# A hybrid decoder layer: mixer and filling work emitted step by step, with the q, k, v and pool projections woven into the top-key search

## The chip, the core and the metric

The kernel runs on one core of a Trainium2 chip. The metric is device microseconds of one execution. The core has five engines that matter here: TensorE (PE in the profile, with its weight loads as PEld), VectorE (DVE), ScalarE (ACT), GpSimd (POOL) and SyncE (SP), which issues most of the DMAs. The engines run side by side, each through its own queue in order, and meet at semaphores.

## What is computed

One layer over 1,024 tokens of width 1,024, in float32:

```python
x = x + 0.5 * swiglu(rms_norm(x, ffn1_norm), ffn1_w_gate, ffn1_w_up, ffn1_w_down)   # width 2816
h = rms_norm(x, mix_norm)
q, k, v, qi, ki, wi, u = split(h @ w_in)           # 512, 512, 512, 256, 64, 4, 512 columns
q, k = rope(rms_norm(q)), rope(rms_norm(k))        # 8 heads of 64
score[t, s] = sum_h wi[t, h] * relu(qi[t, h] . ki[s])   # 4 index heads, causal
attn = softmax attention of each query over its 256 best keys by score
pooled = (trailing mean over 2/4/8/16 tokens - token) @ pool_w * pool_scale   # 4 channel groups, from u
x = x + concat(attn, pooled) @ w_out
x = x + 0.5 * swiglu(rms_norm(x, ffn2_norm), ffn2_w_gate, ffn2_w_up, ffn2_w_down)
```

## The kernel before, in words

The 1,024 tokens are worked on in two halves of 512. Every float32 operand of a matmul is split into a high and a low part, and a product is three matmuls (`mm3`, lines 65 to 68; all of them are recorded under line 63). The parts are made by `split`: a copy on ScalarE and a subtraction on VectorE or GpSimd.

The program goes through these stages (lines 797 to 816):

1. The first FFN's gate and up products for both halves at once (`norm_blocks`, `expand`), with the mixer's weights split beside them into DRAM pieces (`make_piece`).
2. `down(0)`: the first FFN's down projection of half 0, alone. In groups of four 128-wide slices of the hidden width, `down_group` (line 354) loads and splits weights, and sums twelve matmuls into a bank of the tag `fg` for each of four token tiles and two column halves.
3. `mixer(0, "A")`, the mixer of half 0.
4. `norm_transposed(0, 2, "A")`, the norm ahead of the second FFN of half 0.
5. `down(1)`, 6. `mixer(1, "B")`, 7. the norm of half 1, 8. `ffn(0)`, the whole second FFN of half 0, 9. `ffn(1)`.

A mixer (line 772) does, in this order: a transposing norm into four buffers `XA` or `XB` (two for the high parts, two for the low ones); the index projection with its rotary step (`index_proj`); the scores of those token tiles that have more than 256 keys to choose from (`scores`; two tiles in half 0, four in half 1); the pooling mixer (`pool_mixer`); the projections of v, k and q (`v_proj`, `qk_proj`), which go to DRAM; the search for the 256th best score (`top_masks`); attention; the output projection (`out_proj`).

`proj` (line 449) takes four PSUM banks, two of the tag `ba` and two of `bt`, one for each token tile, and for each of eight weight pieces does 12 matmuls. `qk_proj` copies each bank into an `sc` tile, computes the norm over each head and rotates: line 511 multiplies by the norm on GpSimd, 513 by the cosine on VectorE, 514 and 515 by the sine on GpSimd, 516 adds on GpSimd; line 519 transposes on TensorE.

`top_masks` is a bitwise search, 31 steps one after the other: half of the tiles are counted against a threshold on VectorE (`count`, line 621) and half on ScalarE (line 641), and two small VectorE operations (647, 648) make the next threshold. In each softmax step of attention (line 699) two tiles of 128 queries are scored, the mask added, exponentiated on ScalarE (715) and scaled on VectorE (719); the transposes and products with v of a step (`values`) are emitted one step later. Each finished head pair is split and written to DRAM (lines 762 to 768), and `out_proj` reads all of it back in four pairs of 128 rows, the attention's last pair as the last.

What sets the order: the program is written for a tile framework. Each tile has a tag with a number of buffers (`BUFS`, `PBUFS`, lines 46 to 48: `sc` 4, `mk` 6, `bw` 3, `XA` 4, `XB` 4, `x8` 4, `ba` 2, `bt` 2, `fg` 3, `pv` 1), and waits where none is free. The framework orders the instructions at compile time by a simulated time line; an instruction emitted earlier has priority, and `high_priority` lifts one above the rest. `split_shared` (line 337) gives the subtraction to VectorE where `alone[0]` is set, otherwise two of three to GpSimd; `ffn` does likewise at line 423.

Of the kernel before, what the change touches and what calls it, by code (L numbers as in the profile page):

```python
# [37 lines left out]
def hybrid_layer(ctx: ExitStack, tc: tile.TileContext, x, ffn1_norm, ffn1_w_gate, ffn1_w_up,  # L38
# [111 lines left out]
    def norm_transposed(h, which, region):  # L150
        hT = [t("X" + region, [128, 4, HALF], F32R) for j in range(4)]
        xn = [normed(h, i) for i in range(4)]
        for k in range(NK):
            ps = bank(("ba", "bt")[k % 2])
# [199 lines left out]
    def down_group(h, gr, acts, wd, scale, done=None):  # L354
        n = len(gr)
        for c in range(2):
            cols = slice(c * 512, (c + 1) * 512)
            wts = down_weights(wd, gr, c)
            for i in range(4):
# [10 lines left out]
                if done is not None and gr[-1] == NF - 1:  # L370
                    r0 = h * HALF + i * 128
                    nc.sync.dma_start(done[0, r0:r0 + 128, cols], xo)

    def down(h, a_in, wd):
        for gr in GROUPS:
# [8 lines left out]
            down_group(h, gr, acts, wd, 1.0)  # L384


    def ffn(h, hT, wg, wu, wd, done):
# [18 lines left out]
        for gr in GROUPS:  # L406
            acts = []
            for ff in range(gr[0], gr[-1] + 1, 2):
                s2 = []
                for pg in expand2(ff, wg):  # L410
# [3 lines left out]
                    s2.append(s)  # L414
                if pend is not None:
                    down_group(*pend)
                    pend = None
                for s, pu in zip(s2, expand2(ff, wu)):
# [5 lines left out]
                    acts.append(a)  # L424
            pend = (h, gr, acts, wd, 0.5, done)
        down_group(*pend)


    def out_proj(h, region):
        fetch_x(h)  # L430
        mt = [None] * 4
        for j in (2, 3, 0, 1):
            mt[j] = t("X" + region, [128, 2, 2, HALF], F32R)
            nc.gpsimd.dma_start(mt[j].rearrange("p k l c -> p k (l c)"),
                                m_dr[h][2 * j:2 * j + 2].rearrange("k p l c -> p k (l c)"))
        for c in range(2):
            banks = [bank(tag, "op") for tag in ("ba", "ba", "bt", "bt")]
            for n, k in enumerate((4, 5, 6, 7, 0, 1, 2, 3)):
                wt = get_piece(P_O + 2 * k + c)
                m = mt[k // 2][:, k % 2]  # L440
                for i in range(4):
                    tok = slice(i * 128, (i + 1) * 128)
                    mm3(banks[i], m[:, 0, tok], m[:, 1, tok], wt[:, 0], wt[:, 1], n == 0, n == NK - 1)
# [5 lines left out]
    def proj(hT, first, n):  # L449
        hi, lo = hT  # L450
        banks = [bank(tag, "pj") for tag in ("ba", "ba", "bt", "bt")]
        for k in range(NK):
            wt = get_piece(first + k, n)
            for i in range(4):
                tok = slice(i * 128, (i + 1) * 128)
                mm3(banks[i][:, :n], hi[k][:, tok], lo[k][:, tok], wt[:, 0], wt[:, 1], k == 0, k == NK - 1)
# [7 lines left out]
    def index_proj(h, hT, cs):  # L464
        banks = proj(hT, P_I, N_I)
        for i in range(4):
# [29 lines left out]
            nc.vector.tensor_sub(k2[64:], pk[64:], f(k2[64:]))  # L496

    def qk_proj(h, hT, cs, which):
        banks = proj(hT, P_QKV + 8 * which, 512)
        for i in range(4):  # L500
# [5 lines left out]
            nc.scalar.copy(s[:, 512:], banks[i])  # L506
# [4 lines left out]
            nc.gpsimd.tensor_mul(n, n, r[:, :, None].to_broadcast([128, NH, HD]))  # L511
# [4 lines left out]
            nc.gpsimd.tensor_add(o, o, m)  # L516
# [6 lines left out]
            for l, v in enumerate((hi, lo)):  # L523
# [4 lines left out]
                nc.sync.dma_start(dst.rearrange("a p c -> p a c"), f(v).rearrange("p (a c) -> p a c", a=4))  # L528

    def v_proj(h, hT):  # L530
        banks = proj(hT, P_QKV + 16, 512)
        for i in range(4):
# [3 lines left out]
            for l, v in enumerate((hi, lo)):  # L536
                nc.sync.dma_start(v_dr[h * HALF + i * 128:h * HALF + (i + 1) * 128, :, l], f(v).rearrange("p (h d) -> p h d", d=HD))

    def pool_mixer(h, hT):
        hi, lo = hT  # L540
        tiles = []
        for g in range(4):
# [38 lines left out]
            nc.sync.dma_start(m_dr[h][4 + g], f(m))  # L581

    def scores(h, i, sc):
# [5 lines left out]
        for c0 in range(0, n2, 512):  # L589
            cw = min(512, n2 - c0)  # L590
            o = sc[:, c0:c0 + cw]
            for hd in range(4):
# [6 lines left out]
                else:  # L599
                    r = t("mk", [128, 512])  # L600
                    nc.scalar.activation(r[:, :cw], b[:, :cw], AF.Relu)
                    nc.vector.scalar_tensor_tensor(o, r[:, :cw], w, o, op0=ALU.mult, op1=ALU.add)
        d = sc[:, g * 128:(g + 1) * 128]
        nc.vector.scalar_tensor_tensor(d, diag, DIAG, d, op0=ALU.mult, op1=ALU.add)

    def top_masks(h, tiles, sc, masks):
# [32 lines left out]
        for bit in range(30, -1, -1):  # L639
# [5 lines left out]
            for j in range(d):  # L645
# [3 lines left out]
                                           op1=ALU.bitwise_xor)  # L649
        nc.vector.tensor_scalar(th[:, act], f(c[:, act]), -1.0, None, op0=ALU.mult)  # L650
# [10 lines left out]
        for j in range(m):  # L661
# [7 lines left out]
            if n2 > n:  # L669
                nc.gpsimd.memset(masks[j][:, n:n2], NEG)  # L670

# [7 lines left out]
    def attention(h, masks, region):  # L679
# [19 lines left out]
        def softmax(hd, ql, nk, ks, qt):  # L699
# [18 lines left out]
            for ti in range(2):  # L718
# [135 lines left out]
```

## Time and profile before

| | |
|---|---|
| time of three runs | 2051.86, 2048.58, 2051.59 us (median 2051.59) |
| the profiled execution's own time | 2051.53 us |
| its span, first to last instruction | 2049.7 us |
| mean granted TensorE clock | 0.967 |
| busy, TensorE | 1913.4 us |
| busy, VectorE / ScalarE / GpSimd | 1146.2 / 800.6 / 648.9 us |

The span is what the rows of the profile add up to; the time of the execution is 1.8 us longer. Rows of the kind "stage" give the length of a stretch of the span, the busy time of an engine in it with its number of instructions, and the clock granted to TensorE; the length less the busy time is that engine's idle time.

### The profile page before, as it was taken

What the parts mean: (1) busy time and instruction counts of PE and PEld (TensorE: products, weight loads), DVE (VectorE), ACT (ScalarE), POOL (GpSimd) and SP (SyncE); (2) the same over time, 40 slices, a digit from 0 to 9 for tenths busy, and PEclk for the clock granted to TensorE, in tenths of its full rate; (3) what the DMA queues carried; (4) which work ended last, traced back from release to release, by engine and by line L of the source; (5) the groups of instructions that cost most, each with busy time, mean ns of one, the idle gap of its engine ahead of it and who ended that gap; (6) DMA issues with size and microseconds to landing.
All of it is one profiled execution on the core that took longest, in us unless ns stands there. A gap on an engine that the chain in (4) does not pass through costs nothing.

```text
span 2049.7 us, 24399 instructions
## 1 busy us (share of the span) xinstructions
PE 1913.4 (93%) x8640; PEld 1566.5 (76%) x8640; DVE 1146.2 (56%) x2038; ACT 800.6 (39%) x1490; POOL 648.9 (32%) x609
## 2 busy tenths in 40 slices
PE   4999999999999999748799999999999889999999
PEld 2788888887888777536588888787888668888887
DVE  7656656654564693357133689536768523444344
ACT  6343333332333352235143377433565413222331
POOL 6545545520022451752123333675332010000000
PEclk8999999999999999969899999999999899999999
DMA  4366656657455547677536337485555433333332
GB/s 127 114 199 202 206 157 198 220 197 280 136 193 171 137 131 211 206 133 196 188 99 170 101 100 227 127 229 137 134 134 164 145 124 102 91 95 93 92 113 72
DMA packets 223050, 315.26 MB, mean 154 GB/s; under 512 B 34128, under 2 KB 141776, under 8 KB 222928
## 3 DMA queue, kind: packets, MB, share of 16 engines
q1 hardware_dynamic: 204304, 281.19, 43.5%
q0 software_dynamic: 18624, 32.51, 7.6%
q8 instruction: 68, 1.11, 0.2%
q14 instruction: 54, 0.44, 0.1%
HBM read 242.84 MB, written 70.81 MB: 153 GB/s over the span
## 4 chain that ended last, share of the span: by engine, by line
PE 72%; DVE 10%; ACT 5%; POOL 5%; issue 4%; DMA 3%; SPq 0%; POOLq 0%; ACTq 0%; DVEq 0%
PE fg L63 28%; PE dn L63 18%; PE bt L63 6%; PE ba L63 5%; PE pv L63 4%; PE pj L63 4%; PE op L63 3%; ACT x L641 2%; DVE x L622 2%; PE tp L733 1%; PE lg L63 1%; PE pu L63 1%; DVE sel L647 1%; DMA rawd<-in_ffn_w_down_dram 1%; POOL st L137 1%
## 5 line engine op out<-in xcount | busy, mean ns | idle before, releaser
L63 PE MATMUL dn<-wd,a 128*128 128x512 f32 x2112 | 510.1, 396 | 10.4 <-DVE x L367 4.5
L63 PEld LDWEIGHTS dn<-wd,a 128*128 128x128 f32 x2112 | 397.8, 190 | 98.5 <-DVE x L367 7.4
L63 PE MATMUL fg<-XA,w 128*128 128x512 f32 x1056 | 261.4, 395 | 0.1
L63 PE MATMUL fg<-XB,w 128*128 128x512 f32 x1056 | 243.0, 391 | 0.1
L63 PEld LDWEIGHTS fg<-XB,w 128*128 128x128 f32 x1056 | 199.1, 189 | 41.7 <-ACT XB L159 0.5
L63 PEld LDWEIGHTS fg<-XA,w 128*128 128x128 f32 x1056 | 196.9, 189 | 40.5 <-ACT XA L159 0.5
L165 ACT CAST w<-rawe 128x512 fp32r<-128x512 f32 x176 | 109.2, 622 | 211.0 <-PE fg L63 137.1
L166 DVE TENSOR_TENSOR w<-x,w 128x512 fp32r<-128x512 f32 x110 | 114.8, 1046 | 104.6 <-ACT w L165 104.1
L165 ACT CAST wd<-rawd 128x512 fp32r<-128x512 f32 x176 | 107.9, 621 | 156.5 <-PE dn L63 107.4
L166 DVE TENSOR_TENSOR w<-rawe,w 128x512 fp32r<-128x512 f32 x115 | 86.2, 754 | 99.8 <-ACT w L165 92.0
L166 DVE TENSOR_TENSOR wd<-rawd,wd 128x512 fp32r<-128x512 f32 x122 | 91.4, 756 | 67.0 <-ACT wd L165 64.0
L166 POOL TENSOR_TENSOR w<-rawe,w 128x512 fp32r<-128x512 f32 x61 | 80.0, 1316 | 146.0 <-ACT w L165 145.7
L166 POOL TENSOR_TENSOR p<-praw,p 128x512 fp32r<-128x512 f32 (+1 forms) x56 | 72.5, 1295 | 144.1 <-ACT p L165 144.1
L367 DVE TENSOR_TENSOR x<-dn,x 128x512 f32<-128x512 f32 x96 | 64.1, 687 | 91.3 <-PE dn L63 91.0
L166 POOL TENSOR_TENSOR wd<-rawd,wd 128x512 fp32r<-128x512 f32 x54 | 74.6, 1387 | 116.8 <-ACT wd L165 116.6
L63 PE MATMUL fg<-B,w 128*128 128x512 f32 x396 | 97.4, 399 | 12.9 <-DVE w L166 6.8
L369 DVE SCALAR_TENSOR_TENSOR x<-dn,x 128x512 f32<-128x512 f32 x96 | 64.8, 688 | 73.3 <-PE dn L63 73.0
L63 PEld LDWEIGHTS fg<-B,w 128*128 128x128 f32 x396 | 75.8, 192 | 30.4 <-DVE w L166 7.5
L63 PE MATMUL pj<-bw,XA 128*128 128x512 f32 (+1 forms) x384 | 88.6, 384 | 6.3 <-DMA bw<-p_dr 5.2
L63 PE MATMUL ba<-B,w 128*128 128x512 f32 x396 | 93.7, 389 | 0.0
L165 ACT CAST w<-x 128x512 fp32r<-128x512 f32 x110 | 66.9, 619 | 57.6 <-PE bt L63 23.2
L63 PE MATMUL pj<-bw,XB 128*128 128x512 f32 (+1 forms) x384 | 85.5, 372 | 2.4 <-ACT sc L555 1.2
(242 smaller groups left out, 3193.3 us busy)
## 6 DMA issues: line engine op xcount, KB each, us to landing
bw<-p_dr SPq DMA_DIRECT2D x96, 512.0 KB, 4.0
rawd<-in_ffn_w_down_dram SPq DMA_DIRECT2D x88, 512.0 KB, 3.9
p_dr<-p SPq DMA_DIRECT2D x96, 256.0 KB, 2.7
rawe<-in_ffn_w_gate_dram SPq DMA_DIRECT2D x44, 512.0 KB, 4.0
rawe<-in_ffn_w_up_dram SPq DMA_DIRECT2D x44, 512.0 KB, 3.9
x<-in_ffn_w_gate_dram SPq DMA_DIRECT2D x22, 512.0 KB, 4.9
x<-in_ffn_w_up_dram SPq DMA_DIRECT2D x22, 512.0 KB, 6.4
a_dr<-sc SPq DMA_DIRECT2D x44, 256.0 KB, 4.9
```

Source lines behind the costliest of these rows:

```text
L63: nc.tensor.matmul(o, lhs, rhs, start=start, stop=stop, skip_group_check=goes_on)
L137: nc.gpsimd.tensor_tensor(r[:, :n], r[:, :n], mhalf[:, :n], op=ALU.pow)
L165: nc.scalar.copy(hi, src)
L166: eng.tensor_sub(lo, src, f(hi))
L367: nc.vector.tensor_add(xo, ps, xo)
L369: nc.vector.scalar_tensor_tensor(xo, ps, scale, xo, op0=ALU.mult, op1=ALU.add)
L622: nc.vector.tensor_scalar(masks[j][:, :ns[j]], sc[j][:, :ns[j]], thr, None, op0=op, op1=ALU.add, accum_out=cnt[:, j:j + 1])
L641: nc.scalar.activation(masks[j][:, :ns[j]], sc[j][:, :ns[j]], AF.Sign, bias=f(c[:, j:j + 1]), accum_out=cnt[:, j:j + 1])
L647: nc.vector.tensor_tensor(taken, cnt, goal, op=ALU.is_lt)
L733: nc.tensor.transpose(tp[:, j * 128:(j + 1) * 128], sm[ti][:, (2 * k2 + kk) * 128:(2 * k2 + kk + 1) * 128], ident)
```

## The change

Every long function becomes a generator that yields after each small step. What it yields is a number: how many microseconds of filling work are to be emitted behind that step. `fill(main, other)` runs the mixer and draws steps of the filling work by these numbers; `both` alternates the projections' steps with those of the search, 2.2 of the latter for each of the former; `rest` emits what is left. Besides:

- k and q are now projected first, then v, then the pooling mixer, and the search is emitted in between;
- lines 511 and 516 go from GpSimd to VectorE, and the first copy of a q or k bank gets high priority;
- one of the two softmax scalings goes to ScalarE;
- the last head pair's parts go to `out_proj` as SBUF tiles, and the other seven rows are loaded in order 4 to 7, 0 to 2;
- in half 0 the two score tiles are in an `XB` buffer instead of two `sc` buffers;
- `alone` is set before the rest of `ffn(0)` is emitted, not behind it.

The diff's core:

```diff
-        xn = [normed(h, i) for i in range(4)]
+        xn = []
+        for i in range(4):
+            xn.append(normed(h, i, home))
+            yield 2.0
         for k in range(NK):
...
+            yield 0.8
...
     def down_group(h, gr, acts, wd, scale, done=None):
...
+                yield 0.68 * n
...
     def ffn(h, hT, wg, wu, wd, done):
...
                     s2.append(s)
+                    yield 5.4
                 if pend is not None:
-                    down_group(*pend)
+                    yield from down_group(*pend)
                     pend = None
...
                     acts.append(a)
+                    yield 5.4
...
-    def out_proj(h, region):
+    def out_proj(h, region, last):
         fetch_x(h)
-        mt = [None] * 4
-        for j in (2, 3, 0, 1):
-            mt[j] = t("X" + region, [128, 2, 2, HALF], F32R)
-            nc.gpsimd.dma_start(mt[j].rearrange("p k l c -> p k (l c)"),
-                                m_dr[h][2 * j:2 * j + 2].rearrange("k p l c -> p k (l c)"))
+        mt = {}
+        for k in (4, 5, 6, 7, 0, 1, 2):
+            if k % 2 == 0:
+                pair = t("X" + region, [128, 2, 2, HALF], F32R)
+                n = 1 if k == 2 else 2
+                nc.gpsimd.dma_start(pair[:, :n].rearrange("p k l c -> p k (l c)"),
+                                    m_dr[h][k:k + n].rearrange("k p l c -> p k (l c)"))
+            mt[k] = [pair[:, k % 2, l] for l in range(2)]
+        mt[3] = last
         for c in range(2):
...
+                yield 0.0
             for i in range(4):
                 xo = x_at(h, i)[:, c * 512:(c + 1) * 512]
                 nc.vector.tensor_add(xo, banks[i], xo)
+            yield 1.0
...
     def qk_proj(h, hT, cs, which):
...
-            nc.scalar.copy(s[:, 512:], banks[i])
+            with tc.high_priority(offset=HIGH):
+                nc.scalar.copy(s[:, 512:], banks[i])
...
-            nc.gpsimd.tensor_mul(n, n, r[:, :, None].to_broadcast([128, NH, HD]))
+            nc.vector.tensor_mul(n, n, r[:, :, None].to_broadcast([128, NH, HD]))
...
-            nc.gpsimd.tensor_add(o, o, m)
+            nc.vector.tensor_add(o, o, m)
...
+            yield 0.0
...
     def scores(h, i, sc):
...
+                yield 0.55
...
             nc.vector.reciprocal(st[:, :, 4:5], st[:, :, 3:4])
-            for ti in range(2):
-                nc.vector.tensor_scalar(sm[ti], sm[ti], st[:, ti, 4:5], None, op0=ALU.mult)
+            nc.scalar.mul(sm[0], sm[0], st[:, 0, 4:5])
+            nc.vector.tensor_scalar(sm[1], sm[1], st[:, 1, 4:5], None, op0=ALU.mult)
...
                     if pend is not None:
                         pend()
+                    yield 2.2
...
                             split(parts[0], parts[1], mo, nc.gpsimd)
+                            if hp == 3:
+                                return parts
...
-        pend()
-
+        last = pend()
+        yield 4.0
+        return last
+
+    def both(a, b, ratio):
+        due = 0.0
+        for want in a:
+            yield want
+            due += ratio
+            while due >= 1.0:
+                due -= 1.0
+                w = next(b, None)
+                if w is not None:
+                    yield w
+        yield from b
...
+    def fill(main, other):
+        due = 0.0
+        while True:
+            try:
+                due += next(main)
+            except StopIteration as e:
+                return e.value
+            while due > 0.0:
+                got = next(other, None)
+                if got is None:
+                    due = 0.0
+                else:
+                    due -= got
...
     def mixer(h, region):
...
-        pool_mixer(h, hT)
-        v_proj(h, hT)
-        qk_proj(h, hT, cs, 1)
-        qk_proj(h, hT, cs, 0)
         for i in range(4):
             if i not in todo:
                 causal_mask(i, masks[i])
-        top_masks(h, todo, [sc[i] for i in todo], [masks[i] for i in todo])
-        attention(h, masks, region)
-        out_proj(h, region)
+        yield from both(chain(qk_proj(h, hT, cs, 1), qk_proj(h, hT, cs, 0), v_proj(h, hT), pool_mixer(h, hT)),
+                        top_masks(h, todo, [sc[i] for i in todo], [masks[i] for i in todo]), 2.2)
+        last = yield from attention(h, masks, region)
+        yield from out_proj(h, region, last)
...
     alone[0] = False
-    mixer(0, "A")
-    hT0 = norm_transposed(0, 2, "A")
-    down(1, a_dr, ffn1_w_down)
-    mixer(1, "B")
-    hT1 = norm_transposed(1, 2, "B")
+    other = down(1, a_dr, ffn1_w_down)
+    fill(mixer(0, "A"), other)
+    hT0 = fill(norm_transposed(0, 2, "A"), other)
     w2 = (ffn2_w_gate, ffn2_w_up, ffn2_w_down)
-    ffn(0, hT0, *w2, out)
+    rest(other)
+    other = ffn(0, hT0, *w2, out)
+    fill(mixer(1, "B"), other)
+    hT1 = fill(norm_transposed(1, 2, "B"), other)
     alone[0] = True
-    ffn(1, hT1, *w2, out)
+    rest(other)
+    rest(ffn(1, hT1, *w2, out))
```

The steps of `index_proj`, `v_proj`, `pool_mixer` and `top_masks` yield 0.0. Steps of `both` yield what the projections and the search yield, so nothing is drawn there.

More of the change, by code (lines that the diff above doesn't have):

```diff
@@ L148, in normed, with norm_transposed @@
         return xi
-    def norm_transposed(h, which, region):
+    def norm_transposed(h, which, region, home="sc", tags=("ba", "bt")):
         hT = [t("X" + region, [128, 4, HALF], F32R) for j in range(4)]
-        xn = [normed(h, i) for i in range(4)]
+        xn = []
+        for i in range(4):
+            xn.append(normed(h, i, home))
+            yield 2.0
         for k in range(NK):
-            ps = bank(("ba", "bt")[k % 2])
+            ps = bank(tags[k % 2])
             for i in range(4):
@@ L383, in down @@
                 acts.append(a)
-            down_group(h, gr, acts, wd, 1.0)
+            yield from down_group(h, gr, acts, wd, 1.0)
     def ffn(h, hT, wg, wu, wd, done):
@@ L446, in out_proj, with proj @@
                 nc.vector.tensor_add(xo, banks[i], xo)
-    def proj(hT, first, n):
+            yield 1.0
+    def proj(hT, first, n, rounds=(("ba", "ba", "bt", "bt"),)):
         hi, lo = hT
[L451 to L456, printed above, removed]
+        banks = []
+        for tags in rounds:
+            some = [bank(tag, "pj") for tag in tags]
+            for k in range(NK):
+                wt = get_piece(first + k, n)
+                for i, b in enumerate(some, len(banks)):
+                    tok = slice(i * 128, (i + 1) * 128)
+                    mm3(b[:, :n], hi[k][:, tok], lo[k][:, tok], wt[:, 0], wt[:, 1], k == 0, k == NK - 1)
+            banks += some
         return banks
@@ L581, in pool_mixer @@
             nc.sync.dma_start(m_dr[h][4 + g], f(m))
+            yield 0.0
     def scores(h, i, sc):
@@ L670, in top_masks @@
                 nc.gpsimd.memset(masks[j][:, n:n2], NEG)
+            yield 0.0
     def causal_mask(i, m):
@@ L766, in pend, with chain, rest @@
                             split(parts[0], parts[1], mo, nc.gpsimd)
+                            if hp == 3:
+                                return parts
                             for l in range(2):
                                 nc.sync.dma_start(m_dr[h][hp, :, l], f(parts[l]))
-        pend()
+        last = pend()
[12 more added lines that the diff above has]
+        yield from b
+    def chain(*parts):
+        for p in parts:
+            yield from p
+    def fill(main, other):
[11 more added lines that the diff above has]
+                    due -= got
+    def rest(other):
+        for _ in other:
+            pass
     def mixer(h, region):
-        hT = norm_transposed(h, 1, region)
+        hT = yield from norm_transposed(h, 1, region)
         park_x(h)
         cs = rope_tables(h)
-        index_proj(h, hT, cs)
+        yield from index_proj(h, hT, cs)
         masks = t("x8", [128, 4, S], BF16)
@@ L779, in mixer @@
         todo = [i for i in range(4) if 4 * h + i >= 2]
-        sc = {i: t("sc", [128, S]) for i in todo[:2]}
-        if len(todo) > 2:
-            more = t("x8", [128, 2, S])
-            sc.update({i: more[:, j] for j, i in enumerate(todo[2:])})
-        for i in todo:
-            scores(h, i, sc[i])
-        pool_mixer(h, hT)
-        v_proj(h, hT)
-        qk_proj(h, hT, cs, 1)
-        qk_proj(h, hT, cs, 0)
+        sc = {}
+        for n, i in enumerate(todo):
+            if h and n < 2:
+                sc[i] = t("sc", [128, S])
+            else:
+                if n % 2 == 0:
+                    two = t("x8" if h else "XB", [128, 2, S])
+                sc[i] = two[:, n % 2]
+        for i in todo:
+            yield from scores(h, i, sc[i])
         for i in range(4):
```

11 lines of the change are left out of this document (7 added, 4 removed).

## The prediction

> **What bounds the kernel now.** I read the page's totals and slices first.
>
> ```profile
> span 2049.7 us, 24399 instructions
> PE 1913.4 (93%) x8640; PEld 1566.5 (76%) x8640; DVE 1146.2 (56%) x2038; ACT 800.6 (39%) x1490; POOL 648.9 (32%) x609
> ...
> PE   4999999999999999748799999999999889999999
> ...
> PEclk8999999999999999969899999999999899999999
> ```
>
> TensorE is busy for 1913.4 of 2049.7 us. The change removes no matmul, so all that it can win is idle time of TensorE, 136.3 us, plus a little clock. The slices place the idle time: the start, slices 16 to 19 (820 to 1025 us), and a shallow dip at slices 31 and 32. So I cut the span at the stages of the two mixers and asked for TensorE alone in each (columns: length, busy us and matmuls, granted clock, DMA share, GB/s).
>
> ```profile
> 600.00:690.00 90.00, 87.94 (x435) 0.98 0.62 184
> 690.00:776.00 86.00, 80.15 (x340) 0.97 0.44 143
> 776.00:830.00 54.00, 53.67 (x233) 0.98 0.62 178
> 830.00:865.00 35.00, 27.86 (x118) 0.90 0.76 251
> 865.00:906.00 41.00, 9.65 (x35) 0.56 0.67 138
> 906.00:966.00 60.00, 49.37 (x253) 0.90 0.79 187
> 966.00:1028.00 62.00, 48.23 (x203) 0.88 0.51 173
> 1028.00:1182.00 154.00, 154.00 (x740) 0.99 0.45 125
> 1182.00:1304.00 122.00, 119.64 (x526) 1.00 0.52 161
> 1304.00:1404.00 100.00, 99.26 (x451) 1.00 0.68 179
> 1404.00:1580.00 176.00, 172.77 (x890) 0.98 0.53 132
> 1580.00:1632.00 52.00, 42.89 (x242) 0.90 0.47 161
> 1632.00:1690.00 58.00, 50.14 (x209) 0.91 0.44 145
> ```
>
> Length less busy time is the idle time. The first seven rows (the mixer of the first half) give 2.1 + 5.9 + 0.3 + 7.1 + 31.4 + 10.6 + 13.8 = 71.1 us; the last six (the mixer of the second half) 0 + 2.4 + 0.7 + 3.2 + 9.1 + 7.9 = 23.3 us. The other 41.9 us of the 136.3 lie where the change does nothing (start, first FFN, last FFN). So 94.4 us is the most that order can give.
>
> Why is the first mixer emptier? Its filling work is the down projection of half 1: 22 x 3 x 4 x 2 = 528 matmuls. The next view is its matmuls (tile dn) in the same stages.
>
> ```profile
> 600.00:690.00 90.00, 59.05 (x239) 0.98 0.62 184
> 690.00:776.00 86.00, 46.61 (x181) 0.97 0.44 143
> 776.00:830.00 54.00, 26.04 (x108) 0.98 0.62 178
> 830.00:865.00 35.00, 6.12 (x26) 0.90 0.76 251
> ```
>
> These are 554, the last 26 or so of half 0 among them: the filling work is gone by 835 us, and everything after it in that mixer runs bare. It was emitted behind the whole mixer and still ran inside it. So the compile-time scheduler takes any ready instruction for an idle engine, and emission order is a priority, not an order. That is the fact on which my sum turns. The second mixer has ffn(0) as filling, 1,584 matmuls, which lasts to about 1580 us, and only its last two rows are thin.
>
> What does TensorE wait for in the bare stretch? The waits from 820 to 1035 us say it (total, times, longest):
>
> ```profile
> PE qt L519 <- POOL qk L516: 24.0, 5, 9.9
> PE op L63 <- DMA XA<-m_dr: 8.6, 1, 8.6
> ```
>
> The first is the transposes of q, last of the projections, behind GpSimd's chain of normalisation and rotary; the second is the output projection behind the last head pair's trip through DRAM.
>
> **The change, part by part.** *Order of the projections.* k and q now come ahead of v and pool, so q's chain on GpSimd runs beneath v and pool.
>
> ```profile
> 2023.21 10.88 PE fg L63 x48
> L63 PE MATMUL pu<-XA,bw x96: 387/389/579, 648.7 to 716.9; 128*128 128x512 f32 x96
> L63 PE MATMUL pu<-XB,bw x96: 387/389/579, 1078.6 to 1199.3; 128*128 128x512 f32 x96
> ```
>
> At 10.88/48 = 0.227 us a matmul, v's 96 and pool's 96 are 43.5 us, more than the 41 us of the stage 865 to 906, so the 24.0 us of waits for q go. What is late next: the XA buffers hold the transposed input until pool's last matmul, and only then can the first keys load.
>
> ```profile
> L687 POOL DMA_DIRECT2D XA<-k_dr x8: 592/602/676, 872.1 to 925.6; - x8
> ...
> DMA to landing us min/median/max: 4.7/7.0/16.2
> ```
>
> One issue and one landing are 0.6 + 7.0 = 7.6 us, and I leave 8 us idle of the 38.5 (7.1 + 31.4) in 830 to 906: **30.5 us gained**. The bounds are 4.7 + 0.6 and 16.2 + 0.6 us of idle, that is 33 to 22 us gained.
>
> *Weaving with the search.* The search stays a chain between ScalarE and VectorE of 31 steps; its steps now stand between those of k, q, v and pool instead of behind them.
>
> ```profile
> L641 ACT ACTIVATE x<-sc,sel x31: 719/725/727, 703.4 to 770.8; 128x512 bf16<-128x512 f32 x31
> ```
>
> In the first mixer it ran from 703 to 771 us, ahead of the bare stretch. Now each step's count on ScalarE is a wait in VectorE's queue with operations of k and q behind it, and the transposes behind those; k and q delay the search in turn. v and pool lie behind all of it as cover. In 690 to 776 us TensorE idles 5.9 us already, with filling; between 5.9 us gained and as much lost I take zero.
>
> *GpSimd to VectorE.* Two operations of each q or k tile change engine.
>
> ```profile
> L511 POOL TENSOR_TENSOR qk<-qk,st x16: 1035/1046/1066, 818.8 to 1394.1; 128x512 f32<-128x512 f32 x16
> L513 DVE TENSOR_TENSOR qk<-qk,st x16: 675/694/1758, 819.9 to 1396.2; 128x512 f32<-128x512 f32 x16
> L516 POOL TENSOR_TENSOR qk<-qk,qm x16: 1262/1286/1307, 830.2 to 1397.5; 128x512 f32<-128x512 f32 x16
> ```
>
> GpSimd loses 1.046 + 1.286 = 2.33 us a tile, 37 us in all; VectorE, by its own operation of that shape at L513, gains 2 x 0.694 = 1.39 us, 22 us in all (2 x 1.758 = 3.5 us a tile at worst). The chain is 0.9 us a tile shorter, but it is covered now, so I count zero; if the cover fails it is worth 4 x 0.9 = 4 us in the bare stretch. The Trainium skill, in "Perfetto Trace Analysis", section "Optimizing Scalar/DVE Operations", speaks against this edit: the two engines share an SBUF read port, so moving operations between them might not help. By it the 4 us would be nothing; the 1.758 us maximum of L513 against its 0.694 median agrees that something slows VectorE at times, and the sum stands either way.
>
> *Softmax scale.* One of each two scalings goes from VectorE to ScalarE.
>
> ```profile
> 906.00:966.00 60.00, 49.82 (x152) 0.90 0.79 187
> L719 DVE TENSOR_SCALAR p<-p,sm x64: 335/606/1775, 901.4 to 1621.0; 128x256 f32<-128x256 f32 x16, 128x512 f32<-128x512 f32 x16, 128x768 f32<-128x768 f32 x16, 128x1024 f32<-128x1024 f32 x16
> ```
>
> VectorE is busy 49.82 of 60 us in the attention of the first mixer, so it is what that stage leans on. Sixteen of its 32 scalings at 0.335 us or a little more are some 6 us. I take **2 us gained** of the 10.6 idle (bounds 0 and 6), because ScalarE is in the same chain.
>
> *Output projection.* The last head pair goes from its SBUF tile straight into the matmuls, and the others load without waiting for it; its two tiles stay in `mk` buffers until then, and only scratch of the next norm waits for those. The 8.6 us wait goes, **8.5 us gained**. Next late is the transposing norm, about 5 us, with filling only if some is left.
>
> ```profile
> 989.42 29.48 PE L63 MATMUL op<-bw,XA 128*128 128x512 f32 x120 [8.59 <-DMA XA<-m_dr]
> ```
>
> These 120 matmuls took 29.48 us where 120 x 0.227 = 27.2 us would do, after an idle stretch with the clock at 0.88. With the long gaps gone, such matmuls speed up: **3 us gained** over both mixers, bounds 0 and 6. The Trainium skill ("TensorE: Matmul & The Clock Gate", Part 1) says that idling for some 3.4 us halves the clock; the 0.56 of 865 to 906 agrees, and no term is taken from it.
>
> *Filling emitted in steps.* By the yields, the first mixer and the norm behind it ask for 14.4 + 4.4 + 39.2 + 2 + 14.4 = 74 us of the 120 us of down(1). But emission is only priority: whenever a projection waits for a weight piece or a bank, ready filling goes out. Pool's 22 us move behind v, so still more filling is spent before the search. I expect none left for attention, and count zero there.
>
> *A side effect.* In the second mixer the steps ask for 14.4 + 17.6 + 39.2 + 2 + 14.4 = 88 us of ffn(0)'s 1,584 x 0.227 = 359 us. The other three quarters are emitted after `alone` was set, so their splits all go to VectorE instead of one in three.
>
> ```profile
> 1684.00:2049.00 365.00, 86.88 (x127) 1.00 0.31 93
> 1182.00:1304.00 122.00, 112.09 (x282) 1.00 0.52 161
> ```
>
> The first row is those splits on VectorE beneath ffn(1): 0.684 us each. Of ffn(0)'s 132 splits, 0.75 x 88 = 66 move: 45 us, and some 11 us of activation residues. VectorE is at 112 of 122 us in the search (second row), so the search gets longer, while the projections no longer follow it; from 1182 us to the first logits I expect about the 220 us of before. TensorE has filling all through. If the mixer's chain grows by the whole 56 us, ffn(0) is used up that much earlier and the bare tail grows by 56 us at its present idle share, 9.1/52: 10 us lost. If it shrinks by as much, 10 us gained. I take zero, and 5 us gained of the 7.9 in 1632 to 1690 from the direct last pair.
>
> **Sum.** 30.5 + 2 + 8.5 + 3 + 5 = 49 us. The profiled execution took 2051.53 us (span 2049.7), the median of the runs is 2051.59: 2051.5 - 49 = 2002.5, forecast **2003 us**. Its own range by the bounds is 1980 to 2028.
>
> **Rivals.** *Filling is kept back.* If priorities do leave down(1) to attention and the norms, the first mixer's idle falls from the 30 us that I leave to some 7, and the second's from 18 to 4: 2003 - 37 = 1966 us. For it: steps name 53 us for attention and norm alone. Against: dn's rows. Chance 0.17.
>
> *The scheduler goes its own way.* It reordered thousands of instructions before, and if v and pool still run first, only the local edits count: 4 + 8.5 + 5 = 17 us, 2034 us. Chance 0.13.
>
> *Pool is slow, and now it is last.* Its matmuls are 22 us but took 68 us in the first mixer (648.7 to 716.9) and 121 us in the second, held by banks and buffers that ScalarE, GpSimd and VectorE free. Then nothing hung on it; now the XA buffers do, and with them the first keys. At 68 us the gap becomes 68 - 22 + 8 = 54 us, against 38.5 now: 15.5 us lost; in the second mixer attention starts some 50 us later at the tail's idle share: 9 us lost; with 8.5 and 5 us gained, 2051.5 + 11 = 2063 us. It decides from a stretch of about 50 us on, first to last pu, at which the gap is no shorter than now. For it: both rows. Against: at its new place the search is nearly over and scores hold no banks. Chance 0.15.
>
> *No net change.* Terms of both signs cancel, 2051 us: 0.05.
>
> **How the numbers follow.** The forecast has 0.50. Faster by over 0.2% (4 us, about what a measurement of this kernel can tell): 0.50 + 0.17 + 0.13 = 0.80; within it 0.05; slower 0.15. The range from 1962 to 2050 holds the forecast and the first two rivals, and leaves out the slow case and the no-change case, 0.20.
>
> **What would show it.** Right: waits of qt for GpSimd near zero; first logits of the first mixer some 30 us earlier; dn gone before them; no wait of op for m_dr above 3 us; ffn(0)'s first matmul some 41 us earlier; attention's stage still with idle gaps. Wrong: dn running inside attention (first rival); pu ahead of q's matmuls (second); pu from first to last over 50 us behind v, and TensorE bare beneath it (third); the tail of the second mixer bare for over 100 us (side effect mis-sized).

## The result, and the profile after

The changed kernel takes 1988.84 us (median of four runs, 1987.68 to 1994.31) where the kernel before takes 2050.59 on the same chip: a ratio of 0.9705, with a 95% interval from 0.9685 to 0.9725. It is 62 us faster; 49 were forecast. The profiled execution is the slowest of the four (1994.31 us), so each stretch of its trace may be a few microseconds long.

The page of the kernel after, its totals and the two rows of slices:

```profile
span 1992.5 us, 24277 instructions
...
PE 1897.6 (95%) x8640; PEld 1558.0 (78%) x8640; DVE 1166.1 (59%) x2119; ACT 818.6 (41%) x1520; POOL 515.7 (26%) x496
...
PE   4999999999999699988999999999999899999999
...
PEclk8999999999999799998999999999999999999999
```

TensorE's idle time is 1992.5 - 1897.6 = 94.9 us, 41.4 less than before, and its busy time is 15.8 us less. Two new things stand out: the dip at slices 16 to 19 is nearly gone, and there is one at slice 13, which wasn't there before. GpSimd has lost 133 us of work; VectorE, which took most of it over, is busy only 19.9 us longer.

TensorE alone by stages of the kernel after (length, busy us and matmuls, granted clock, DMA share, GB/s); the last row is the whole second mixer with its filling:

```profile
600.00:640.00 40.00, 40.00 (x221) 1.00 0.53 176
640.00:680.00 40.00, 22.25 (x80) 0.70 0.60 175
680.00:776.00 96.00, 92.39 (x407) 0.98 0.60 193
776.00:830.00 54.00, 52.97 (x238) 1.00 0.88 246
830.00:870.00 40.00, 35.76 (x146) 0.91 0.42 120
870.00:930.00 60.00, 50.02 (x265) 0.91 0.84 212
930.00:989.00 59.00, 52.71 (x247) 0.98 0.65 226
...
989.00:1625.00 636.00, 625.49 (x3023) 0.99 0.53 151
```

The first mixer idles 42.9 us instead of 71.1, and 17.75 of these are the new hole at 640 to 680. The second idles 10.5 us instead of 23.3. The bare stretch of before (830 to 906, 38.5 us idle) has become 14.2 us in 830 to 930. What runs there is filling, as the matmuls of the tile dn alone show in the kernel after:

```profile
640.00:680.00 40.00, 3.70 (x15) 0.70 0.60 175
...
830.00:870.00 40.00, 34.45 (x131) 0.91 0.42 120
870.00:930.00 60.00, 12.49 (x50) 0.91 0.84 212
```

So 47 us of the down projection of half 1 run after 830 us, beside attention, whose first logits start at 835.7 us. The prediction expected none there. In the hole nearly none run. The waits from 600 to 1030 us of the kernel after (total, times, longest) say what TensorE stands for:

```profile
PE ba L63 <- DMA qm<-qi_dr: 11.6, 2, 10.3
...
PE qt L539 <- DVE qk L536: 1.9, 1, 1.9
PE op L63 <- DMA bw<-p_dr: 1.6, 2, 1.0
```

The 24.0 us of the transposes of q are 1.9, and the output projection no longer waits for `m_dr` at all. The longest wait was 2.1 us before: the index scores wait for their loads at a time when there is no filling.

For comparing kernels I cut each trace at the first matmul of `ffn(0)` and the first of `ffn(1)`. These are rows of the tile fg in the kernel after (min/median/max ns, first and last start):

```profile
L63 PE MATMUL fg<-XA,w x1056: 387/389/796, 989.5 to 1520.5; 128*128 128x512 f32 x176
...
L63 PE MATMUL fg<-XB,w x1056: 387/389/794, 1624.8 to 1976.4; 128*128 128x512 f32 x176
```

Before, they began at 1026.3 and 1681.8 us. So the part up to the end of the first mixer gained 36.8 us, and the second mixer shrank from 655.5 to 635.3 us, another 20.2. The part behind it takes 366.9 to 368.5 us in every kernel here.

### The profile page after: what moved, and what is told of

The parts are those of the page before. It is cut to its first block, busy times and chain, and to the rows that moved or that the text cites. A ratio compares the mean times of both kernels' runs of the same rounds, so it can differ in the third digit from the quotient of the medians.

```text
span 1992.5 us, 24277 instructions
## 1 busy us (share of the span) xinstructions
PE 1897.6 (95%) x8640; PEld 1558.0 (78%) x8640; DVE 1166.1 (59%) x2119; ACT 818.6 (41%) x1520; POOL 515.7 (26%) x496
## 4 chain that ended last, share of the span: by engine, by line
PE 85%; DVE 5%; DMA 3%; POOL 2%; ACT 2%; issue 2%; SPq 0%; POOLq 0%; ACTq 0%; DVEq 0%
PE fg L63 32%; PE dn L63 22%; PE bt L63 6%; PE pj L63 6%; PE ba L63 5%; PE pv L63 5%; PE op L63 4%; PE pu L63 2%; PE tp L759 2%; PE lg L63 1%; DMA bw<-p_dr 1%; POOL st L137 1%; ACT x L665 1%; DMA rawd<-in_ffn_w_down_dram 1%; DMA qm<-qi_dr 1%
## 5 line engine op out<-in xcount | busy, mean ns | idle before, releaser
L63 PE MATMUL dn<-wd,a 128*128 128x512 f32 x2112 | 506.5, 394 | 8.0 <-DVE wd L170 3.0
L170 DVE TENSOR_TENSOR w<-rawe,w 128x512 fp32r<-128x512 f32 x158 | 110.2, 704 | 119.7 <-ACT w L169 114.6
L170 DVE TENSOR_TENSOR w<-x,w 128x512 fp32r<-128x512 f32 x110 | 109.9, 1001 | 105.5 <-ACT w L169 105.1
L170 DVE TENSOR_TENSOR wd<-rawd,wd 128x512 fp32r<-128x512 f32 x144 | 105.4, 739 | 56.6 <-ACT wd L169 53.8
L170 POOL TENSOR_TENSOR p<-praw,p 128x512 fp32r<-128x512 f32 (+1 forms) x56 | 72.4, 1293 | 137.8 <-ACT p L169 137.7
L169 ACT CAST w<-x 128x512 fp32r<-128x512 f32 x110 | 66.8, 618 | 59.7 <-PE bt L63 23.3
L169 ACT CAST p<-praw 128x512 fp32r<-128x512 f32 (+1 forms) x56 | 33.5, 598 | 136.0 <-DMA praw<-in_w_in_dram 60.9
L63 PEld LDWEIGHTS ba<-B,w 128*128 128x128 f32 x396 | 74.3, 188 | 15.4
```

What stands on the lines that cost most here:

```text
L63: nc.tensor.matmul(o, lhs, rhs, start=start, stop=stop, skip_group_check=goes_on)
L169: nc.scalar.copy(hi, src)
L170: eng.tensor_sub(lo, src, f(hi))
```

## The experiments

Each had three timed rounds beside the kernel before, which took 2048.9 to 2049.9 us there. "First" is the start of `ffn(0)` and "second" the time from there to the start of `ffn(1)`, both from one profiled execution; the medians are of four runs or more. The kernels were timed on several chips, so a difference of a microsecond or two between rows says nothing.

| kernel | median us (range) | ratio to before, interval | first | second |
|---|---|---|---|---|
| before | 2050.59 (2048.58 to 2051.86) | 1 | 1026.3 | 655.5 |
| after | 1988.84 (1987.68 to 1994.31) | 0.9705 [0.9685, 0.9725] | 989.5 | 635.3 |
| after, old order | 2002.84 (2001.65 to 2004.55) | 0.9778 [0.9763, 0.9792] | 998.5 | 635.7 |
| after, no weaving | 1990.03 (1984.34 to 1993.12) | 0.9711 [0.9691, 0.9731] | 980.0 | 635.3 |
| after, no steps | 1994.79 (1992.24 to 2000.04) | 0.9746 [0.9728, 0.9764] | 988.8 | 634.3 |
| after, `alone` late | 2006.25 (2001.53 to 2007.22) | 0.9789 [0.9774, 0.9804] | 985.3 | 651.5 |
| after, q and k on GpSimd | 2009.1 (2008.02 to 2010.44) | 0.9802 [0.9787, 0.9817] | 995.9 | 644.0 |
| after, last pair by DRAM | 2004.68 (2002.9 to 2008.97) | 0.9783 [0.9769, 0.9798] | 996.2 | 638.0 |
| before, new order | 2048.15 (2044.11 to 2051.75) | 0.9994 [0.9985, 1.0004] | 1015.6 | 662.2 |
| before, work off GpSimd | 2020.5 (2018.29 to 2021.91) | 0.9857 [0.9842, 0.9872] | 1003.8 | 645.9 |
| before, both | 2014.62 (2013.97 to 2016.52) | 0.9831 [0.9816, 0.9845] | 1005.1 | 639.3 |
| after, early buffer | 1983.4 (1982.84 to 1984.34) | 0.9676 [0.966, 0.9692] | 979.7 | 635.1 |
| and masks free | 1990.41 (1988.22 to 1991.28) | 0.9707 [0.9691, 0.9724] | 986.0 | 636.2 |
| and all on VectorE | 1979.66 (1979.15 to 1980.44) | 0.9659 [0.9645, 0.9673] | 975.1 | 634.4 |

### One part undone at a time

**The old order**, with the search behind the projections, as it was:

```diff
-        yield from both(chain(qk_proj(h, hT, cs, 1), qk_proj(h, hT, cs, 0), v_proj(h, hT), pool_mixer(h, hT)),
-                        top_masks(...), 2.2)
+        yield from chain(pool_mixer(h, hT), v_proj(h, hT), qk_proj(h, hT, cs, 1), qk_proj(h, hT, cs, 0))
+        yield from top_masks(...)
```

> The changed kernel with the projections again emitted as pool, v, k, q and the whole search behind them; steps of filling work, engine moves and the direct last pair are kept. Theory A (order: v and pool are the cover of q's chain, some 30 us in the first mixer; how filling is emitted is worth about nothing): 2010 to 2025 us, with waits of the q transposes back. Theory B (paced filling work is the gain): within 8 us of the changed kernel's 1989.

It cost 14 us, between the two theories; by the profiles 9.0 us lie in the first mixer and 0.4 in the second. The waits of q's transposes did not come back, as theory A had it: they are 0.3 us in both mixers together. The old order puts these transposes at 812.7 to 875.0 us, and dn ran to 874, so they had filling beneath them this time. What TensorE waits for instead is q's load ahead of the first logits, 5.6 us. **No weaving**: the new order, with the search behind it.

```diff
-        yield from both(chain(...), top_masks(...), 2.2)
+        yield from chain(qk_proj(h, hT, cs, 1), qk_proj(h, hT, cs, 0), v_proj(h, hT), pool_mixer(h, hT))
+        yield from top_masks(...)
```

> The changed kernel with k, q, v, pool in the new order but the whole search emitted behind them instead of woven in. Theory A (weaving itself is worth zero): within 6 us of 1989. Rival (weaving is what lets attention start early): 2001 us or more, with the search ending later in both mixers.

1.2 us, inside the interval: weaving is worth nothing that can be measured. **No steps**: no filling is drawn while the mixer is emitted.

```diff
-                due += next(main)
+                due += 0.0 * next(main)
```

> The changed kernel with what each step asks for multiplied by zero, so that each mixer and the norm behind it are emitted whole and all filling work behind them, as before. Theory A: within 8 us of 1989, since ready filling work goes out early either way. Theory B: 2004 to 2025 us, with the down projection's matmuls used up some 50 us before attention of the first mixer.

It cost 6 us, and dn still ran to about 890 us. So it isn't the steps that keep filling for attention. The edit does a second thing: all of `ffn(0)` is now emitted behind `alone`, and 29 more operations go from GpSimd to VectorE (2148 instead of 2119). The 6 us are the steps' worth less what that gives back, and no run separates the two. **`alone` late**: the rest of `ffn(0)` is emitted before `alone` is set, so two of three of its splits go to GpSimd again.

```diff
-    alone[0] = True
     rest(other)
+    alone[0] = True
```

> The changed kernel with alone set behind the rest of ffn(0), as before, so that GpSimd again does two of three of ffn(0)'s splits beneath the second mixer. As predicted (a longer VectorE queue and a freer one cancel): within 6 us of 1989. Theory C (GpSimd's relief makes VectorE's other work faster, and that is part of the gain): 1999 us or more, with VectorE's other operations longer in the mean.

It cost 17 us, and its second mixer is 16.2 us longer. The totals on the page of this kernel, to be held against those of after:

```profile
PE 1898.8 (95%) x8640; PEld 1556.3 (78%) x8640; DVE 1151.7 (57%) x2038; ACT 819.8 (41%) x1520; POOL 624.6 (31%) x577
```

Setting it early adds 81 operations to VectorE (2038 to 2119) and only 14.4 us, and takes 109 us from GpSimd. **The two operations of q and k** back on GpSimd:

```diff
-            nc.vector.tensor_mul(n, n, r[:, :, None].to_broadcast([128, NH, HD]))
+            nc.gpsimd.tensor_mul(n, n, r[:, :, None].to_broadcast([128, NH, HD]))
...
-            nc.vector.tensor_add(o, o, m)
+            nc.gpsimd.tensor_add(o, o, m)
```

> The changed kernel with the two operations of each q or k tile back on GpSimd (multiply by the norm, add after rotation). As predicted (the chain is covered by v and pool): 1987 to 1993 us. Theory C (GpSimd's relief counts, as setting alone late cost 17 us): 37 us of GpSimd work come back in the two searches, 1997 us or more, with the transposes of q and k waiting for GpSimd.

It cost 20 us, by the profiles in both mixers (6.4 and 8.7 us). The transposes of q wait no longer for that: 0.1 us in all. In the first mixer a wait of po for the last operation of pool's chain, L596, has grown from 0.9 to 5.4 us. So the two operations cost time, but not by the wait for q that theory C named. **The last head pair by DRAM**, loaded with the others:

```diff
-        for k in (4, 5, 6, 7, 0, 1, 2):
+        for k in (4, 5, 6, 7, 0, 1, 2, 3):
...
-        mt[3] = last
```

> The changed kernel with the last head pair again written to DRAM and read back for the output projection. As predicted (8.5 us in the first mixer, 5 us in the second): about 2002 us, with a wait of op for m_dr of 8 us or so in the first mixer. Rival (the trip is hidden by the other seven rows and by weight pieces): within 4 us of 1989.

It cost 16 us, and the output projection waits 7.3 us for `m_dr` in the first mixer again, where the prediction had 8.6, and 3.3 us in the second. The profiles show less than the medians, 6.7 and 2.7 us in the two mixers; that of the kernel after is its slowest execution.

The undone parts add up to 14 + 1 + 6 + 17 + 20 + 16 = 74 us, more than the 62 of the whole, so they depend on each other. The next three start from the other end.

### Order alone, relief of GpSimd alone, both

**The new order in the kernel before**, and nothing else:

```diff
-        pool_mixer(h, hT)
-        v_proj(h, hT)
         qk_proj(h, hT, cs, 1)
         qk_proj(h, hT, cs, 0)
+        v_proj(h, hT)
+        pool_mixer(h, hT)
```

> The kernel before with one edit: k, q, v, pool in place of pool, v, k, q, the search still behind. As the prediction had it (order alone is worth 30 us in the first mixer): 2018 to 2024 us. After the run with the old order, which cost 14 us: about 2036 us. Rival (order needs the other edits, since filling work is gone by then): 2045 us or more.

It changed nothing: 0.9994. The first mixer gained 10.7 us, and the second lost 6.7. The waits of this kernel from 600 to 1030 us:

```profile
PE dn L63 <- DVE x L367: 6.9, 1, 6.9
PE pu L63 <- DVE mk L535: 6.7, 1, 6.7
PE op L63 <- DMA XA<-m_dr: 6.6, 1, 6.6
PE po L63 <- DVE sc L572: 5.1, 1, 5.1
PE po L63 <- DVE sc L574: 5.0, 1, 5.0
```

The waits of q are gone, as forecast. In their place stand those of the pooling mixer: po waits for VectorE's last operations on the windowed sums, which come from a chain of additions on GpSimd. Filling is used up at about 825 us (836 before), so pool's chain now runs as bare as q's did.

**Work off GpSimd in the kernel before**, nothing else. This goes further than the change: the splits of the down projection of half 1 move too.

```diff
-            nc.gpsimd.tensor_mul(n, n, r[:, :, None].to_broadcast([128, NH, HD]))
+            nc.vector.tensor_mul(n, n, r[:, :, None].to_broadcast([128, NH, HD]))
...
-            nc.gpsimd.tensor_add(o, o, m)
+            nc.vector.tensor_add(o, o, m)
...
-    alone[0] = False
```

> The kernel before with nothing but work moved off GpSimd: the two operations of q and k on VectorE, and all splits and residues of down(1) and ffn(0) too. If the two edits are worth what undoing them cost (20 and 17 us) by themselves: 2005 to 2020 us. Rival (they pay only with the new order): 2035 to 2050 us, and the wait of q's transposes stays, now for VectorE.

29 us faster, without a change of order or filling and half a microsecond above the first range on record. Of the two waits that the prediction read in the kernel before, the second is still there, and the first has only changed its engine (820 to 1035 us):

```profile
PE qt L519 <- DVE qk L516: 20.2, 4, 7.6
PE op L63 <- DMA XA<-m_dr: 8.5, 1, 8.5
```

So the gain didn't come from the wait for q, which fell by 3.8 us only. What did change is how long VectorE's other operations take. The page's totals of this kernel, and two lines of its code (min/median/max ns):

```profile
PE 1899.7 (94%) x8640; PEld 1561.6 (77%) x8640; DVE 1194.8 (59%) x2224; ACT 799.9 (40%) x1490; POOL 415.6 (21%) x423
```

```profile
L647 DVE TENSOR_TENSOR sel<-sel x62: 148/160/629, 702.3 to 1272.0; 128x2 int32<-128x2 f32 x31, 128x4 int32<-128x4 f32 x31
...
L713 DVE TENSOR_SCALAR sm<-sm x32: 144/160/661, 877.6 to 1583.6; 128x2 f32<-128x2 f32 x32
```

The same two lines in the kernel before:

```profile
L647 DVE TENSOR_TENSOR sel<-sel x62: 146/163/1257, 705.6 to 1293.5; 128x2 int32<-128x2 f32 x31, 128x4 int32<-128x4 f32 x31
...
L713 DVE TENSOR_SCALAR sm<-sm x32: 149/167/3092, 897.0 to 1617.5; 128x2 f32<-128x2 f32 x32
```

Read the three numbers together. Minimum and median are the same; the maximum has about halved, or fallen further. Most of these tiny operations were never delayed, but some stood still. Whom they stood behind is to be seen by setting a long one beside what GpSimd does at that time, in the kernel before (start, duration); first one of L647, then the longest of L713:

```profile
725.97 1.26 DVE L647 TENSOR_TENSOR sel<-sel 128x2 int32<-128x2 f32 x1
725.45 1.76 POOL L166 TENSOR_TENSOR wd<-rawd,wd 128x512 fp32r<-128x512 f32 x1
```

```profile
1556.91 3.09 DVE L713 TENSOR_SCALAR sm<-sm 128x2 f32<-128x2 f32 x1
1558.68 1.29 POOL L166 TENSOR_TENSOR mo<-o,mo 128x512 fp32r<-128x512 f32 x1
```

The VectorE operation ends at 727.23 us and the GpSimd operation at 727.21; in the second pair it is 1560.00 and 1559.97. This holds for every long one. Of the 216 operations of L644, L647, L648 and L713 in the kernel before, 39 took over 0.5 us, and each of the 39 ended 14 to 36 ns after an operation of GpSimd had ended. Of the 175 that took under 0.3 us, one ended within 40 ns after one. In this kernel 9 operations over 0.5 us are left. The means fell from 321 to 177 ns (L647) and from 420 to 184 ns (L713).

GpSimd lost 233 us here, VectorE took 186 operations over, and its busy time grew by only 48.6 us. The operations that VectorE runs equally often in both kernels last 51 us less in sum. Such small operations stand in the chains that TensorE waits for, but how the 29 us are made up is not shown. In the first mixer the search, from its first to its last count on ScalarE, fell from 67 to 60 us; in the second it did not (105 and 107). Two other causes are in the edit besides, and no run takes them apart: the moved operations are themselves shorter on VectorE, and what stays on GpSimd has less ahead of it in GpSimd's queue.

**Both together**, in the kernel before:

> The kernel before with the new order of the projections, which changed nothing alone (ratio 0.9994), and the work of the run above moved off GpSimd. Theory (the order pays only when GpSimd's work is off pool's chain): at least 14 us faster than the run above. Rival (order is worth nothing without filling that lasts): within 5 us of the run above.

5.9 us faster than relief alone: between the two expectations. The order is worth nothing without relief and 6 us with it, the other parts still missing; its gain is in the second mixer this time (645.9 to 639.3). In the first, po still waits 5.1 and 5.0 us for the same two operations as with the new order alone, L572 and L574.

### The new hole

The cause is read from the loads that SyncE issues, here those of `rawa`, the activations of the down projection (start, duration). First the kernel after from its seventh load on, the first of half 1; the second line stands for four loads, the first three at 658 to 660 us. Then the kernel before from its eighth:

```profile
528.10 0.37 SPq L383 DMA_DIRECT2D rawa<-a_dr  x1
658.62 20.30 SPq L383 DMA_DIRECT2D rawa<-a_dr  x4
```

```profile
552.36 0.37 SPq L378 DMA_DIRECT2D rawa<-a_dr  x1
...
609.62 0.37 SPq L378 DMA_DIRECT2D rawa<-a_dr  x1
647.28 0.37 SPq L378 DMA_DIRECT2D rawa<-a_dr  x1
```

Before, a load went out every 15 to 38 us; after, none between 528 and 658 us. The tile `rawa` of half 1 has the tag `XB`, and so has the changed kernel's buffer for the score tiles of half 0. Buffers of a tag are given out in the order of emission, and the score tiles are emitted ahead of most of the filling. So `rawa` stands behind a buffer that isn't written before the first scores, and the filling stops for want of activations. **The early buffer** takes it before the norm, so that it isn't last in that line:

```diff
+        if not h:
+            two = t("XB", [128, 2, S])
+            nc.vector.memset(two[:, :, :1], 0.0)
...
-                if n % 2 == 0:
-                    two = t("x8" if h else "XB", [128, 2, S])
+                if h and n % 2 == 0:
+                    two = t("x8", [128, 2, S])
```

> The changed kernel with the first half's score buffer taken from XB ahead of the norm (a small memset claims it), so that the activation loads of down(1) no longer queue behind it and need not wait past the index projection. If the new bare stretch of 17 us at 640 to 680 us is lost time: 1972 to 1980 us. Rival (it only keeps filling work back for attention, whose chain sets the end): within 5 us of 1989, with down(1) used up some 17 us earlier and attention barer.

The hole is gone: TensorE is busy for 40.00 of 40 us at 640 to 680. But only 5.4 us came back, not 17. These are this kernel's matmuls of dn alone:

```profile
640.00:680.00 40.00, 30.40 (x129) 1.00 0.66 187
...
830.00:870.00 40.00, 11.60 (x48) 0.75 0.65 202
870.00:930.00 60.00, 0.00 (x0) 0.91 0.74 197
```

Now dn runs out at 847 us, and 830 to 870 idles 16.3 us instead of 4.2. The hole had kept filling back, by accident, for the place where pool's chain is bare. Both theories on record missed the size.

**The masks free.** With the early buffer, the masks of the first mixer are finished only from 847 us on, though the search ends at about 750: their tiles have the tag `mk`, behind those of pool. I gave them another tag.

```diff
-            e, k, s = t("mk", [128, S], BF16)[:, :n], ...
+            e, k, s = t("mk" if h else "t", [128, S], BF16)[:, :n], ...
```

> The kernel with the early buffer (1983.4 us), and the tile that a mask is finished in comes from another tag in the first mixer, so that masks no longer queue behind the pooling mixer's tiles. Theory (the first mixer's attention starts late because its masks wait for those tiles): first transposes of attention some 15 us earlier than 871, 1966 to 1974 us. Rival (attention starts when the first keys have landed, behind pool's last matmul, whatever the masks do): 1980 to 1987 us.

The theory fell: the masks are finished from 764 us on, and the kernel is 7 us slower, outside both ranges on record. q's transposes wait once more for VectorE in this kernel:

```profile
PE qt L539 <- DVE qk L536: 5.9, 1, 5.9
```

Pool's first matmul is 7 us later (811.5 instead of 804.7 us), and so are attention's first transposes. Why attention starts when it does is to be seen on VectorE. These are the last operation of pool's chain (L596) and the first of softmax (L734), with the idle time before each; first the kernel with the early buffer, then this one:

```profile
864.82 0.42 DVE L596 SCALAR_TENSOR_TENSOR sc<-mk,sc 128x256 f32<-128x256 f32 x1 [4.48 <-POOL mk L587]
865.16 0.42 DVE L734 CUSTOM_DVE_ANT_0 p<-lg,x 128x256 f32<-128x256 f32 x1
```

```profile
872.03 0.42 DVE L596 SCALAR_TENSOR_TENSOR sc<-mk,sc 128x256 f32<-128x256 f32 x1 [4.49 <-POOL mk L587]
872.37 0.42 DVE L734 CUSTOM_DVE_ANT_0 p<-lg,x 128x256 f32<-128x256 f32 x1
```

VectorE sat idle for 4.5 us until GpSimd delivered pool's last sum, and the softmax went right behind it without a wait of its own. It had been ready: its logits start at 842.8 and 853.5 us in the two kernels, and the masks end at about 855 and 776. It stood behind in the queue. In these kernels attention of the first mixer starts when pool's chain ends, whatever the masks do. None with the new order put softmax ahead of that chain, so what this is worth wasn't tried.

**All on VectorE**: the same kernel, and no split of the down projection of half 1 or of `ffn(0)` on GpSimd any more.

```diff
-    alone[0] = False
```

> The same, and no split or residue of down(1) and ffn(0) goes to GpSimd: all on VectorE. Theory (work taken off GpSimd makes VectorE's other operations shorter, so it is nearly free): at least 4 us faster than the same kernel without it. Rival (VectorE is full in the first mixer's search and attention, and the added splits delay them): at least 4 us slower.

10.7 us faster than without it, within what the theory of relief expected. It is the fastest kernel of all, 0.9659 of before and about 9 us below the change. Its totals:

```profile
PE 1888.3 (95%) x8640; PEld 1552.6 (79%) x8640; DVE 1179.0 (60%) x2193; ACT 817.1 (41%) x1520; POOL 418.7 (21%) x423
```

VectorE has 73 operations more than with the masks free alone, and is busy 9.8 us longer (1169.2 to 1179.0); GpSimd has lost 100 us (519.0 to 418.7). The same two lines on VectorE stand at 861.35 and 861.70 us: pool's chain ends 10.7 us earlier, and with it all that follows. That this comes from shorter operations on VectorE, as the theory says, is not shown. With the masks free alone, the sums of pool's chain (L587) shared GpSimd's queue with splits (L170):

```profile
842.50 0.64 POOL L587 TENSOR_TENSOR sc<-sc 128x271 f32<-128x271 f32 x1
843.09 1.29 POOL L170 TENSOR_TENSOR wd<-rawd,wd 128x512 fp32r<-128x512 f32 x1
844.34 0.64 POOL L587 TENSOR_TENSOR mk<-sc 128x269 f32<-128x269 f32 x1
```

Here the second sum starts 1.84 us after the first, behind a split; with all splits on VectorE the same two start 0.71 us apart (836.34 and 837.05 us). The search of the first mixer got longer at the same time, from 57 to 70 us on ScalarE, beneath filling.

## Why the prediction was right or wrong

The sum came near (49 us of 62; the median lies inside its own range), but the gain was not where the sum had put it. In large part that is luck: a term of 30.5 us was worth nothing by itself, and two that were counted as nothing were worth 20 and 17 us. The bounds that the prediction states for its terms add up to 1977 to 2032 us, a little more than the 1980 to 2028 that it gives.

**Order, 30.5 us: failed.** The step was "v's 96 and pool's 96 are 43.5 us, more than the 41 us of the stage 865 to 906, so the 24.0 us of waits for q go". They went, but pool's matmuls are not cover: between them stands pool's own chain over GpSimd and VectorE, and it took q's place in the bare stretch. Alone, the order is worth 0. With everything else in place, undoing it costs 14 us, and even then q's transposes wait for 0.3 us only, under filling that the prediction held to be gone. The forecast looked for the next late thing only at the keys' load, 8 us; of the waits on pool's chain the trace of before showed a single one in 600 to 830 us, po for L574, 2.2 us, since the chain lay under filling there.

**GpSimd to VectorE, zero or 4 us: failed**, and so did the **side effect, zero within 10 us**. Undoing them costs 20 and 17 us, and work moved off GpSimd gives 29 us by itself. Both were costed as sums of VectorE's own time: so many operations more at 0.684 or 0.694 us. The runs showed the other side of the sum: what VectorE does besides gets shorter, by 51 us in the kernel before. How much of the 29 us came that way stays open. The row was there, L513 with a median of 694 and a maximum of 1,758 ns, and was used only as a worst price. The Trainium skill's rule that was weighed ("Perfetto Trace Analysis", "Optimizing Scalar/DVE Operations": moving between these two might not help, as they share a port) lets one expect little of the move; here it was worth 20 us. The reason that the rule gives fits the gain: by the Trainium skill's "SBUF — State Buffer", "Who interferes with whom", a VectorE instruction with two SBUF inputs and a GpSimd instruction that reads SBUF shut each other out, and the one that starts later waits for the whole of the other. The 12 long operations of L647, which read two inputs and end with an operation of GpSimd, agree; that a port does it, no run here shows. L713 reads one input, and by that section contends only if it runs in the two-port mode. Its 6 operations over 0.5 us end with one of GpSimd all the same; in which mode they ran is not shown.

**Second mixer, 5 us: 20.2.** Late `alone` gives back 16.2 of it, so this is for the most part the same mis-sized term. The search did get longer there, as feared (105 us from its first to last count on ScalarE before, 129 after), but TensorE had filling through it.

**Direct last pair, 8.5 + 5 us: right.** The wait for `m_dr` went, and undoing it costs 16 us against 13.5.

**Weaving, zero: right** (1.2 us). **Steps, zero: nearly** (6 us, with the second effect named above).

**Clock, 3 us: too small.** TensorE's busy time fell by 15.8 us, and the mean granted clock rose from 0.967 to 0.977. The groups that shrank most are lg (58.4 to 52.5 us), pj (174.1 to 169.8) and dn (510.1 to 506.5).

**Filling gone before attention: wrong.** dn ran to about 888 us. That is the picture of the first rival, yet not for its reason: without any steps dn lasted as long, and with the buffer taken early it ended at 847. The buffer's place in the line of its tag, which neither forecast nor rivals saw, held it back. The first logits came 55 us earlier (890.9 to 835.7), where 30 were expected.

**The rivals.** Pool took 37 us from first to last pu in the first mixer and 35 in the second, below the 50 from which the slow case decides:

```profile
L63 PE MATMUL pu<-XA,bw x96: 387/389/580, 792.8 to 829.8; 128*128 128x512 f32 x96
```

pu stood behind q's matmuls, so the scheduler didn't go its own way either. The scaling of softmax on ScalarE, 2 us, wasn't tried by itself. In the trace the transposes behind it wait 6.0 us for ScalarE over both mixers, where they waited 6.6 us for VectorE, so no gain is to be seen there. The high priority of the first copy of a q or k bank wasn't tried either.

## What to carry to other kernels

When work leaves an engine that runs beside VectorE, cost both halves: what VectorE gets, and what its small chained operations lose in waiting; a median near the minimum with a far maximum is the sign, and the long operations end with one of the other engine. A reordering moves the wait to whatever is last next, so follow that one's whole chain over all engines, and count its matmuls as cover only if they don't wait themselves. A buffer of a shared tag that is emitted early and written late can stop every later user of the tag.

## What the runs showed of the hardware that was not expected

Tiny VectorE operations stood still until an operation of GpSimd ended: all 39 of those over 0.5 us among 216 in the kernel before ended 14 to 36 ns after one. Moving 186 operations from GpSimd to VectorE in the kernel before shortened two of these groups (L647 and L713) from means of 321 and 420 ns to 177 and 184 ns, at unchanged medians of about 160, and added 48.6 us of busy time to VectorE for 233 us taken from GpSimd. The time moved by 29 us, while the wait that the trace named longest fell by 3.8.
